# Two weight blocks at the head of the load queue, and set-up tables issued behind their rounding and subtraction

## The chip, the core and the metric

The kernel runs on one core of a Trainium2 chip. The metric is the device time of one execution in microseconds (us), median over runs. A core has TensorE (PE, matrix products; PEld is its weight load), VectorE (DVE), ScalarE (ACT), GpSimd (POOL) and SyncE (SP). SP issues most loads; ACT and POOL issue some. Each engine works through its own instructions in a fixed order, and an instruction that waits holds up everything behind it on that engine.

## The reference

Two networks follow each other on 256 tokens of width 1024. The first is a block of two layers: a norm, a projection to 3072 columns, differential and block attention, an output projection, and a convolutional feed-forward part. The second has one layer with a recurrent mixer and one with neighbourhood attention, with a second stream of 256 context tokens and modulation vectors that are computed from `w_ada`. What the change touches is the beginning:

```python
for i in range(DEPTH):
    h = rms_norm(x, ln_attn_g[i])
    dq, dk, dv, mq, mk, mv = jnp.split(h @ w_in[i], cuts, axis=-1)
    ...
```

All of it is in float32.

## The kernel before

The tokens stand in two tiles `x[0]` and `x[1]` of 128 tokens. A product of float32 is made of three products of rounded values: an operand is split into `hi` (rounded) and `lo` (the rest), and `hi*hi`, `hi*lo` and `lo*hi` are summed. For the tokens, `norm_T` does this: per token tile two squares with a sum on ACT (`sqj`), a chain of small DVE instructions (`rstd`), the scaling `xn` (one half on DVE, one on ACT), transposes on PE (`nT`), and then `ah` on ACT and `al` on DVE. The transposes for one part of the width need both token tiles. For the weights, `weights` does it: a load `raw` of a block (512 KB in this lane), the rounding `whi` on ACT (L265), and the subtraction `wlo` on DVE or, every second block, on POOL (L269).

`proj` multiplies the tokens by such blocks. The projection of layer 0 has six parts of 512 columns; each takes 4 blocks of 256 rows, 48 matmuls in all (`prj`, L292 to L294).

Around it, `setup_first` and `setup_second` build small tables: `oh`, `fl`, `rb` and `lam` are loads that ACT issues, POOL issues four loads (`b_sink`, `a_w2`, `a_a2`, `a_g2`) and clears `state`. A second lane of work, the context (`context1`), loads blocks of 128 KB of `w_in_even`, and `ada` multiplies blocks of `w_ada` (`adaw`, L778), transposes the result (`adaT`, L784), adds it up on DVE (L786, L787) and transposes two of the sums once more (`adaR`, L798).

The order in which instructions stand on each engine is not written by hand. A scheduler sorts all instructions of the program by priority and by its own estimate of times; `issue_after(i)` keeps what stands under it behind instruction i, and `high_priority()` puts what stands under it ahead. So a change at the start can move instructions far behind it. Loads of SP and ACT share eight counters in turn: a load that takes a counter waits until the load that had it before has landed, and it waits on the engine that issues it.

Of the kernel before, what the change touches and what calls it, by code (L numbers as in the profile page):

```python
# [10 lines left out]
F32 = mybir.dt.float32  # L11
F32R = mybir.dt.float32r
I32 = mybir.dt.int32
AF = mybir.ActivationFunctionType
OP = mybir.AluOpType
# [136 lines left out]
class Lane:  # L152
# [3 lines left out]
    def __init__(self, net, name, counts, named, banks, weights):  # L156
        self.net, self.name, self.counts, self.named = net, name, counts, named
        self.banks, self.weights = banks, weights
# [30 lines left out]
class Net:  # L189
# [67 lines left out]
    def weights(self, L, src, a, b):  # L257


        nc = self.nc  # L260
        raw = L.tile("raw", [128, a, b], F32, "raw")
        for p, ap in (src if isinstance(src, list) else [(slice(0, 128), src)]):
            nc.sync.dma_start(raw[p], ap)
        hi = L.tile("whi", [128, a, b], F32R, "whi")
        nc.scalar.activation(hi, raw, AF.Copy)  # L265
        lo = L.tile("wlo", [128, a, b], F32R, "wlo")
        L.blocks += 1
        eng = nc.gpsimd if L.blocks % L.nth == 0 else nc.vector
        eng.tensor_tensor(lo, raw, hi.bitcast(F32), op=OP.subtract)  # L269
        return hi, lo  # L270

    def plain_rows(self, w):

        return lambda k, a, n0, n: w[k * 128:(k + a) * 128, n0:n0 + n].rearrange("(a p) f -> p a f", p=128)

    def proj(self, L, act, rows, n0, n, ps, k0=0, nk=8, by_tile=False):


        nc = self.nc
        hi, lo = act  # L280
        a = L.weights // 512
        blocks = range(k0, k0 + nk, a)
        ready = {kb: self.weights(L, rows(kb, a, n0, n), a, n) for kb in blocks} if by_tile else {}
        for kb, t in [(kb, t) for t in range(2) for kb in blocks] if by_tile else \
                [(kb, t) for kb in blocks for t in range(2)]:
            if kb not in ready:
                ready[kb] = self.weights(L, rows(kb, a, n0, n), a, n)
            wh, wl = ready[kb]
            for k in range(a):
                ah, al = hi(kb + k, t), lo(kb + k, t)  # L290
                st, en = kb + k == k0, kb + k == k0 + nk - 1
                nc.tensor.matmul(ps[t][:, :n], ah, wh[:, k], start=st, stop=False)  # L292
                nc.tensor.matmul(ps[t][:, :n], ah, wl[:, k], start=False, stop=False)  # L293
                self.last = nc.tensor.matmul(ps[t][:, :n], al, wh[:, k], start=False, stop=en)  # L294
# [259 lines left out]
    def first_layer(self, i, x, act=None):  # L554
        nc, I, L = self.nc, self.I, self.lat
        w_in = self.plain_rows(I["w_in"][i])
        act = act or self.first_norm(i, x)
# [6 lines left out]

        def project(n):
            ps = [L.pA("prj"), L.pA("prj")]
            self.proj(L, act, w_in, n * 512, 512, ps)
            return ps

        def qkv(n, jq):  # L570

            qa, qb = self.pad_q(L)
            self.q_T(L, self.head_norm(L, project(n)), self.qg8[:, 2 * i + jq:2 * i + jq + 1], qa, qb)
            yield
            kT = L.big([128, 4, 256], name="kT")
            self.k_T(L, self.head_norm(L, project(n + 1)), self.col(f"qkg{i}", 2 * jq + 1), kT)
            yield
            ps = project(n + 2)
            v = L.big([128, 2, 512], name="v")
            for t in range(2):  # L580
                nc.scalar.activation(v[:, t], ps[t], AF.Copy)
            yield qa, qb, kT, v
# [95 lines left out]
        act = self.fns(his, los)  # L678
        for n in range(2):
            ps = [L.pA("wo"), L.pA("wo")]  # L680
# [1082 lines left out]
def run(tc, I, out, colw, cstw, keep):  # L1763
    nc = tc.nc
    with ExitStack() as ctx:
        net = Net(tc, I)
        net.pools(ctx)
        net.setup(colw, cstw, keep)
        x = [net.keep([128, D], F32, name=f"x{t}") for t in range(2)]
        for t in range(2):  # L1770
            nc.sync.dma_start(x[t], I["x"][0, t * 128:(t + 1) * 128])
        act=net.first_norm(0, x)
        net.setup_first()
        net.setup_second()
        net.context1()
        net.first_layer(0, x, act)
        net.conv_ffn(0, x)
        net.rest()
        act1=net.first_norm(1, x)
        net.first_layer(1, x, act1)  # L1780
        net.side()
        net.conv_ffn(1, x)
        net.second_block(x)
        net.store_x(x, out[0])
# [38 lines left out]
```

## Time and profile before

| what | us |
|---|---|
| median of 3 runs (2079.45 to 2088.85) | 2084.95 |
| profiled execution, its own time | 2083.04 |
| its span, first to last instruction | 2081.2 |
| PE busy in the span | 1908.7 |

PE is busy in 92% of the span, so the kernel is bound by PE, and time is lost where PE waits. The profile gives the start of each instruction in us from the start of the span.

### The profile page before, as it was taken

To read this page: it belongs to the slowest core of one execution; us is meant where nothing else is said; L and a number is where in the kernel's file an instruction comes from. 1 tells how busy PE (TensorE), PEld (TensorE's weight loads), DVE (VectorE), ACT (ScalarE), POOL (GpSimd) and SP (SyncE) were. 2 spreads that over 40 slices of the span, in tenths; PEclk is the share of its full clock that TensorE was granted. 3 is DMA by queue.
4 is the path that set the end of the run, shared out by engine and by line. 5 is a ranking of instruction groups with operands and counts; after the bars stand their busy time and mean duration, and the time that the engine had idled before them with its cause. 6 is when DMAs were issued, how large, how long until landed. Compare 5 with 4: busy or idle time off the path is not lost. (4 is left out here: it accounts for less than half of the span.)

```text
span 2081.2 us, 37712 instructions
## 1 busy us (share of the span) xinstructions
PE 1908.7 (92%) x14178; PEld 1592.7 (77%) x14178; DVE 1369.1 (66%) x2855; ACT 1025.4 (49%) x1990; POOL 928.4 (45%) x621
## 2 busy tenths in 40 slices
PE   6989999989998889999898888998699989998998
PEld 4567868888665458899797777887599977777997
DVE  5575378856687555786679878557764468656444
ACT  4455455545454435465456553334454454654443
POOL 3235544693232444544545355446255454113453
PEclk9999999999999999999999998899899999998999
DMA  9957455445455565664573334427465526234562
GB/s 341 310 173 232 153 181 167 151 141 169 131 185 178 190 199 168 198 218 152 163 219 103 102 110 150 127 71 235 158 204 177 178 100 220 78 105 154 181 200 73
DMA packets 270815, 351.08 MB, mean 169 GB/s; under 512 B 43150, under 2 KB 195469, under 8 KB 270632
## 3 DMA queue, kind: packets, MB, share of 16 engines
q1 hardware_dynamic: 267992, 343.32, 51.9%
q0 software_dynamic: 1968, 4.33, 0.7%
q8 instruction: 112, 1.84, 0.4%
q10 hardware_dynamic: 672, 1.02, 0.1%
q14 instruction: 71, 0.58, 0.1%
HBM read 334.04 MB, written 14.55 MB: 167 GB/s over the span
## 5 line engine op out<-in xcount | busy, mean ns | idle before, releaser
L269 POOL TENSOR_TENSOR wlo<-raw,whi 128x1024 fp32r<-128x1024 f32 (+2 forms) x408 | 781.7, 1931 | 982.2 <-ACT whi L265 809.2
L265 ACT ACTIVATE whi<-raw 128x1024 fp32r<-128x1024 f32 (+2 forms) x600 | 507.8, 882 | 142.8 <-issue 35.0
L269 DVE TENSOR_TENSOR wlo<-raw,whi 128x1024 fp32r<-128x1024 f32 x192 | 305.4, 1591 | 108.2 <-ACT whi L265 94.2
L308 PE MATMUL f<-ah,whi 128*128 128x256 f32 x768 | 225.8, 294 | 15.2 <-ACT whi L265 14.5
L310 PE MATMUL f<-ah,wlo 128*128 128x256 f32 x768 | 226.8, 295 | 7.6 <-POOL wlo L269 7.6
L309 PE MATMUL f<-al,whi 128*128 128x256 f32 x768 | 225.4, 294 | 0.5 <-DVE al L383 0.5
L746 PE MATMUL acc<-whi,hh 128*128 128x512 f32 x432 | 168.3, 393 | 2.1 <-ACT hh L461 2.1
L747 PE MATMUL acc<-wlo,hh 128*128 128x512 f32 x432 | 169.2, 392 | 0.0
L308 PEld LDWEIGHTS f<-ah,whi 128*128 128x128 f32 x768 | 153.6, 200 | 19.2 <-ACT whi L265 15.7
L748 PE MATMUL acc<-whi,hl 128*128 128x512 f32 x432 | 165.3, 391 | 0.4 <-DVE hl L462 0.4
L310 PEld LDWEIGHTS f<-ah,wlo 128*128 128x128 f32 x768 | 153.7, 200 | 11.7 <-POOL wlo L269 8.7
L309 PEld LDWEIGHTS f<-al,whi 128*128 128x128 f32 x768 | 153.8, 200 | 3.0 <-DVE al L383 0.9
L1584 DVE TENSOR_TENSOR r<-r 128x512 f32<-128x512 f32 x48 | 41.2, 858 | 129.4 <-ACT r L1583 128.3
L1583 ACT ACTIVATE r<-f 128x512 f32<-128x512 f32 x48 | 28.7, 598 | 179.2 <-PE f L310 179.0
L293 PE MATMUL prj<-wlo,ah 128*128 128x512 f32 (+1 forms) x272 | 108.2, 399 | 2.7 <-DVE wlo L269 1.6
L292 PE MATMUL prj<-whi,ah 128*128 128x512 f32 (+1 forms) x272 | 108.9, 406 | 0.4 <-DVE bt L499 0.4
L310 PE MATMUL g<-ah,wlo 128*128 128x256 f32 x352 | 102.1, 290 | 6.3 <-POOL wlo L269 6.3
L294 PE MATMUL prj<-whi,al 128*128 128x512 f32 (+1 forms) x272 | 106.2, 398 | 1.4 <-DVE al L383 1.4
L778 PE MATMUL ada<-adaw,kept 128*32 128x512 f32 x384 | 96.8, 636 | 8.6 <-DMA adaw<-in_w_ada_dram 8.3
L308 PE MATMUL g<-ah,whi 128*128 128x256 f32 x352 | 102.7, 292 | 0.4 <-DVE kept L786 0.4
L310 PE MATMUL up<-ah,wlo 128*128 128x256 f32 x352 | 101.4, 288 | 1.2 <-POOL wlo L269 1.2
L309 PE MATMUL g<-al,whi 128*128 128x256 f32 x352 | 102.3, 291 | 0.0
(473 smaller groups left out, 4861.2 us busy)
## 6 DMA issues: line engine op xcount, KB each, us to landing
raw<-in_w_ff_dram SPq DMA_DIRECT2D x128, 512.0 KB, 4.1
raw<-in_w_up_dram SPq DMA_DIRECT2D x88, 512.0 KB, 4.6
adaw<-in_w_ada_dram SPq DMA_DIRECT2D x144, 256.0 KB, 5.0
raw<-in_w_ff_dram SPq DMA_DIRECT2D x128, 256.0 KB, 3.9
raw<-in_w_in_dram SPq DMA_DIRECT2D x48, 512.0 KB, 4.7
raw<-in_w_down_dram SPq DMA_DIRECT2D x44, 512.0 KB, 4.1
adaw<-in_w_ada_dram SPq DMA_DIRECT2D x24, 512.0 KB, 7.3
raw<-in_w_out_dram SPq DMA_DIRECT2D x24, 512.0 KB, 4.4
```

What stands on the lines that cost most here:

```text
L265: nc.scalar.activation(hi, raw, AF.Copy)
L269: eng.tensor_tensor(lo, raw, hi.bitcast(F32), op=OP.subtract)
L292: nc.tensor.matmul(ps[t][:, :n], ah, wh[:, k], start=st, stop=False)
L293: nc.tensor.matmul(ps[t][:, :n], ah, wl[:, k], start=False, stop=False)
L294: self.last = nc.tensor.matmul(ps[t][:, :n], al, wh[:, k], start=False, stop=en)
L308: nc.tensor.matmul(pv[:, j], wh[:, k % a, c], ah, start=first, stop=False, skip_group_check=skip)
L309: nc.tensor.matmul(pv[:, j], wh[:, k % a, c], al, start=False, stop=False, skip_group_check=skip)
L310: nc.tensor.matmul(pv[:, j], wl[:, k % a, c], ah, start=False, stop=k == 7, skip_group_check=skip)
L746: nc.tensor.matmul(acc[t][n], hh[:, k, c], wh[:, n], start=st, stop=False)
L747: nc.tensor.matmul(acc[t][n], hh[:, k, c], wl[:, n], start=False, stop=False)
L748: self.last = nc.tensor.matmul(acc[t][n], hl[:, k, c], wh[:, n], start=False, stop=en)
L778: nc.tensor.matmul(ps[32 * j:32 * j + 32], self.sT[:, k], raw[:, k - kb], start=k < 4, stop=k >= 4)
```

## The change

`first_weights` takes the first two blocks of the first projection out of `proj` and asks for them with high priority ahead of the set-up. `proj` then finds them in `ready`. `setup_first` is issued after the rounding of the second block (`rounded`, on ACT), `setup_second` after its subtraction (`rest_of`, on POOL).

```diff
+    def first_weights(self):
+        rows, a = self.plain_rows(self.I["w_in"][0]), self.lat.weights // 512
+        with self.tc.high_priority():
+            self.ahead = {kb: self.weights(self.lat, rows(kb, a, 0, 512), a, 512) for kb in range(0, 2 * a, a)}
+        return self.rounded.ins, self.rest_of.ins
...
-        ready = {kb: self.weights(L, rows(kb, a, n0, n), a, n) for kb in blocks} if by_tile else {}
+        ready = {kb: self.weights(L, rows(kb, a, n0, n), a, n) for kb in blocks} if by_tile else ready or {}
...
-            self.proj(L, act, w_in, n * 512, 512, ps)
+            self.proj(L, act, w_in, n * 512, 512, ps, ready=self.ahead if i == n == 0 else None)
...
         act=net.first_norm(0, x)
-        net.setup_first()
-        net.setup_second()
+        rounded, rest_of = net.first_weights()
+        with tc.issue_after(rounded):
+            net.setup_first()
+        with tc.issue_after(rest_of):
+            net.setup_second()
         net.context1()
```

Lines below the new function move by 8 (in `run` by 11). The built program shows what the scheduler makes of it.

The first loads that SP issues, before. `kept` is the place of `x` here, `raw_3411`, `raw_3429`, `raw_3447` and `raw_3465` are the four blocks of the first projection, and `DMAHWn` is counter n.

```order
L1771 DMA kept_58<-in_x_dram 128x1024 x2
L263 DMA raw_459<-in_w_in_even_dram 128x256
L263 DMA raw_3411<-in_w_in_dram 128x2x512
L263 DMA raw_471<-in_w_in_even_dram 128x256 [waits DMAHW0_49]
L263 DMA raw_483<-in_w_in_even_dram 128x256 [waits DMAHW2_49]
L263 DMA raw_3429<-in_w_in_dram 128x2x512 [waits DMAHW3_49]
L263 DMA raw_3447<-in_w_in_dram 128x2x512 [waits DMAHW4_49]
```

The same of the change, where the first two blocks are `raw_155` and `raw_161`.

```order
L263 DMA raw_155<-in_w_in_dram 128x2x512
L263 DMA raw_161<-in_w_in_dram 128x2x512
L1779 DMA kept_58<-in_x_dram 128x1024 x2
L263 DMA raw_471<-in_w_in_even_dram 128x256
L263 DMA raw_483<-in_w_in_even_dram 128x256
L263 DMA raw_495<-in_w_in_even_dram 128x256 [waits DMAHW0_49]
L783 DMA adaw_6655<-in_w_ada_dram 128x512 [waits DMAHW1_49]
L783 DMA adaw_6658<-in_w_ada_dram 128x512 [waits DMAHW2_49]
L263 DMA raw_3447<-in_w_in_dram 128x2x512 [waits DMAHW4_49,DVE_49]
```

The two blocks stand ahead of the tokens, not behind them, and the third block has two loads of `w_ada` ahead of it.

ACT's start before; the first two loads, `cols` and `consts`, stand ahead of these rows in both programs.

```order
L340 ACTIVATE sqj_82,ss_81<-kept_58 128x512 [waits DMAHW1_49]
L340 ACTIVATE sqj_84,ss_81<-kept_58 128x512
L503 DMA lam_217<-in_diff_lambda_dram 128x512
...
L363 ACTIVATE xn_97<-kept_58,rstd_86 128x512 [waits DVE_49]
L340 ACTIVATE sqj_101,ss_100<-kept_58 128x512 [waits DMAHW2_49]
L340 ACTIVATE sqj_103,ss_100<-kept_58 128x512
L475 DMA rb_159<-in_rel_bias_dram 32x12 [waits DMAHW2_49,Activation_49]
L265 ACTIVATE whi_3413<-raw_3411 128x1024 [waits DMAHW6_49]
L363 ACTIVATE xn_116<-kept_58,rstd_105 128x512 [waits DVE_49,Activation_49]
```

ACT's start with the change.

```order
L265 ACTIVATE whi_157<-raw_155 128x1024 [waits DMAHW1_49]
...
L265 ACTIVATE whi_163<-raw_161 128x1024 [waits DMAHW2_49]
L478 DMA oh_167<-in_consts_dram 32x256 [waits DMAHW3_49]
L511 DMA lam_229<-in_diff_lambda_dram 128x512 [waits DMAHW5_49]
L481 DMA fl_169<-in_consts_dram 128x128 [waits DMAHW7_49]
L348 ACTIVATE sqj_82,ss_81<-kept_58 128x512 [waits DMAHW4_49]
...
L265 ACTIVATE whi_473<-raw_471 128x256 [waits DMAHW6_49,Activation_49]
L265 ACTIVATE whi_485<-raw_483 128x256 [waits Activation_49]
L483 DMA rb_171<-in_rel_bias_dram 32x12 [waits DMAHW4_49]
L265 ACTIVATE whi_3449<-raw_3447 128x1024
L371 ACTIVATE xn_116<-kept_58,rstd_105 128x512 [waits DVE_49]
```

Two roundings and three loads now stand ahead of the first square of the tokens. `lam` waits for counter 5, which `x[1]` has, and `fl` for counter 7, which `raw_483` has. `rb` waits for `raw_3447`, and the third block's rounding stands behind it.

PE before, between the last matmuls of the fourth part of the projection (`prj_3779`) and the first of the fifth (`prj_3934`).

```order
L294 MATMUL prj_3779<-whi_3836,al_80 128x512
L528 MATMUL S_3903<-kT_3521,qa_3405 128x128
...
L784 MATMUL adaT_350<-kept_58,asb_348 128x128 x4
L784 MATMUL adaT_6715<-kept_58,asb_6713 128x128 x4
L798 MATMUL adaR_6722<-kept_58 8x128 x2
L370 MATMUL nT_405<-kept_58,xn_382 128x128
L370 MATMUL nT_418<-kept_58,xn_382 128x128
L422 MATMUL qT_3876<-kept_58,hn_3872 128x128 x4
```

The same place with the change.

```order
L302 MATMUL prj_3779<-whi_3836,al_80 128x512
L786 MATMUL ada_6731<-adaw_6744,kept_58 32x512
...
L792 MATMUL adaT_362<-kept_58,asb_360 128x128 x4
L792 MATMUL adaT_6758<-kept_58,asb_6756 128x128 x4
L378 MATMUL nT_417<-kept_58,xn_394 128x128
L378 MATMUL nT_430<-kept_58,xn_394 128x128
L786 MATMUL ada_6765<-adaw_6766,kept_58 32x512
...
L430 MATMUL qT_3876<-kept_58,hn_3872 128x128 x4
```

`adaR` has gone from here to a place some 90 rows earlier, behind eight transposes of `pB`, and nine matmuls of `ada` (four of `ada_6731` and five of `ada_6765`) have come.

## Rows read from the trace of the kernel before

**Rows 1.** The page: span, and busy time of each engine.

```profile
span 2081.2 us, 37712 instructions
PE 1908.7 (92%) x14178; PEld 1592.7 (77%) x14178; DVE 1369.1 (66%) x2855; ACT 1025.4 (49%) x1990; POOL 928.4 (45%) x621
```

**Rows 2.** Timeline of ACT: start, length, engine, line; idle time before in brackets.

```profile
5.19 0.63 ACT L340 ACTIVATE sqj<-kept 128x512 f32<-128x512 f32 x1 [1.76 <-DMA kept<-in_x_dram]
...
10.49 0.19 ACT L340 ACTIVATION_READ_ACCUMULATOR sqj<-kept 128x1 f32 x1
14.89 0.35 ACTq L475 DMA_DIRECT2D rb<-in_rel_bias_dram  x1
15.29 1.06 ACT L265 ACTIVATE whi<-raw 128x1024 fp32r<-128x1024 f32 x1 [4.61 <-DMA raw<-in_w_in_even_dram]
...
21.17 0.41 ACT L265 ACTIVATE whi<-raw 128x256 fp32r<-128x256 f32 x1
```

**Rows 3.** Timeline of all engines, the same stretch.

```profile
16.38 1.23 DVE L269 TENSOR_TENSOR wlo<-raw,whi 128x1024 fp32r<-128x1024 f32 x1 [4.11 <-ACT whi L265]
...
17.71 0.49 DVE L362 TENSOR_SCALAR xn<-kept,rstd 128x512 f32<-128x512 f32 x1
...
19.72 1.22 PE L292 MATMUL prj<-whi,ah 128*128 128x512 f32 x2
```

**Rows 4.** Windows: stretch, length, busy us by engine, PE clock, DMA share, GB/s.

```profile
0.00:3.00 3.00, 0.00 (x0) 0.00 (x0) 0.48 (x1) 0.85 (x1) 2.47 (x9) 1.00 0.36 69
3.00:6.00 3.00, 0.00 (x0) 0.00 (x0) 0.63 (x9) 1.24 (x4) 0.77 (x2) 1.00 1.03 387
6.00:8.50 2.50, 0.00 (x0) 0.00 (x0) 1.85 (x17) 0.72 (x4) 0.00 (x0) 1.00 0.99 201
```

**Rows 5.** Loads of the first 60 us: count, KB each, median us to landing.

```profile
raw<-in_w_in_dram SPq DMA_DIRECT2D x16, 512.0 KB, 6.8
...
adaw<-in_w_ada_dram SPq DMA_DIRECT2D x14, 256.0 KB, 7.1
kept<-in_x_dram SPq DMA_DIRECT2D x2, 512.0 KB, 6.3
...
raw<-in_w_in_even_dram SPq DMA_DIRECT2D x7, 128.0 KB, 8.5
...
kept<-in_consts_dram ACTq DMA_DIRECT2D x1, 336.0 KB
kept<-in_cols_dram ACTq DMA_DIRECT2D x1, 303.0 KB, 4.6
```

**Rows 6.** The tile `raw` in the first 60 us, all its loads.

```profile
DMA to landing us min/median/max: 3.8/7.3/10.7
```

**Rows 7.** Timeline of PE, first part of the projection.

```profile
26.21 1.04 PE L778 MATMUL ada<-adaw,kept 128*32 128x512 f32 x2
...
31.28 0.60 PE L477 MATMUL pB<-oh,rb 32*12 32x256 f32 x2
...
37.69 0.62 PE L292 MATMUL prj<-whi,ah 128*128 128x512 f32 x2
```

**Rows 8.** Timeline, all engines, between the fourth and fifth parts of the projection.

```profile
98.84 1.92 PE L778 MATMUL ada<-adaw,kept 128*32 128x512 f32 x16
...
101.03 0.39 PE L294 MATMUL prj<-whi,al 128*128 128x512 f32 x1
...
104.28 2.27 DVE L396 TENSOR_SCALAR hst<-hst 128x16 f32<-128x16 f32 x1
...
106.96 0.38 PE L798 MATMUL adaR<-kept 128*8 128x128 f32 x2 [3.35 <-DVE kept L787]
...
110.39 1.09 PE L422 MATMUL qT<-kept,hn 128*128 128x128 f32 x4 [1.51 <-DVE rstd L344]
...
113.40 0.63 PE L294 MATMUL prj<-whi,al 128*128 128x512 f32 x1
```

**Rows 9.** Windows: PE's granted clock, as a share of full speed, stands before the DMA share.

```profile
110.00:120.00 10.00, 9.61 (x40) 8.02 (x41) 4.79 (x16) 3.35 (x6) 0.00 (x0) 0.72 0.22 80
```

More of the change, by code (lines that the diff above doesn't have):

```diff
@@ L264, in weights @@
         hi = L.tile("whi", [128, a, b], F32R, "whi")
-        nc.scalar.activation(hi, raw, AF.Copy)
+        self.rounded = nc.scalar.activation(hi, raw, AF.Copy)
         lo = L.tile("wlo", [128, a, b], F32R, "wlo")
@@ L268, in weights, with proj @@
         eng = nc.gpsimd if L.blocks % L.nth == 0 else nc.vector
-        eng.tensor_tensor(lo, raw, hi.bitcast(F32), op=OP.subtract)
+        self.rest_of = eng.tensor_tensor(lo, raw, hi.bitcast(F32), op=OP.subtract)
         return hi, lo
+    def first_weights(self):
[3 more added lines that the diff above has]
+        return self.rounded.ins, self.rest_of.ins
     def plain_rows(self, w):
         return lambda k, a, n0, n: w[k * 128:(k + a) * 128, n0:n0 + n].rearrange("(a p) f -> p a f", p=128)
-    def proj(self, L, act, rows, n0, n, ps, k0=0, nk=8, by_tile=False):
+    def proj(self, L, act, rows, n0, n, ps, k0=0, nk=8, by_tile=False, ready=None):
         nc = self.nc
```

## The prediction

> **What bounds the kernel now.** I read the page first: PE is busy in 1908.7 of 2081.2 us [rows 1], so the time moves only where PE's waits move. Those that the change can reach are at the start, so I went through the timelines of the first 40 us, ACT's first, then DVE's and PE's.
>
> The first matmul of the projection starts at 19.72 [rows 3]. The chain behind it runs as follows. ACT squares the first token tile from 5.19 on and has finished the second tile's squares at 10.49 + 0.19 = 10.68 [rows 2], 5.49 us later. What comes next on ACT is the issue of the small load `rb`, and that comes only at 14.89, since its counter belongs to a load of `w_in_even` that has not landed. ACT stands idle 4.61 us for it, and the rounding of the first weight block starts behind it at 15.29, 1.06 long [rows 2]. DVE has that block's subtraction ahead of the last `rstd` step, so it waits 4.11 us, subtracts for 1.23, and scales the second tile at 17.71 [rows 3]. From there to the first matmul it is 19.72 - 17.71 = 2.01 us. So before, the tokens are early and the weights hold them up: a late `rb` on ACT costs some 4 to 5 us. That is what the change could win.
>
> **The start with the change.** The order shows that the two blocks are loaded ahead of the tokens and not behind them. It also shows that ACT's first square now stands behind the loads `oh`, `lam` and `fl`, and that `fl` waits for the counter of `raw_483`, the eighth load. So the squares start when eight loads have landed: two weight blocks and two token tiles of 512 KB, `cols` with 303, `consts` with 336 and two context blocks of 128 [rows 5], 2943 KB or 3.01 MB. By 3.0 us the core has moved 3 x 69 = 0.21 MB, and then 387 GB/s as long as it has loads in flight [rows 4]. That gives 3.0 + (3.01 - 0.21) / 0.387 = 10.2 us. Between 6.0 and 8.5 the rate before was only 201 GB/s [rows 4], at a time when SP stood waiting for counters. If such a stretch comes back it costs 2.5 x (387 - 201) / 387 = 1.2 us, so 11.4. These are the two bounds. POOL's four loads don't stand in the sum, because they now come behind POOL's first subtraction.
>
> The Trainium skill ("DMA: Bandwidth & Descriptors", section Specifications) gives a core about 358 GB/s from HBM. By it the eight loads would land at an estimated 10.8 us. The rows of this case hold 387 GB/s over 3 us, so the measured rate decides.
>
> From the start of the squares the steps are those of before. The second tile's squares end 5.49 later, at 15.7 to 16.9. ACT rounds two context blocks (0.41 each [rows 2]), which ends at 16.5 to 17.7. Then `rb` is issued, which waits for the third block, `raw_3447`. Ahead of that block on SP stand one more context block and two loads of 256 KB, so 0.13 + 0.52 + 0.52 MB more have to land, and of `lam` and POOL's loads at most another 1 MB. That is 4.2 to 5.2 MB, or 13.3 to 15.9 by the same rate, and 17.1 with the slow stretch: just hidden behind ACT's own work. The rounding of the third block (1.06) then ends at 17.6 to 18.8, and DVE, which again has a subtraction ahead of the scaling, is through 1.23 later, 18.8 to 20.0. With the 0.10 to the scaling and 2.01 to the first matmul it starts at 20.9 to 22.1, which is **1.2 to 2.4 us later than before**. The wait that the change removes from the first block comes back at the third.
>
> What is won is behind that. With the change, the first 48 matmuls of the projection have no `ada` among them. Before, they had six in three pieces of which one is 1.04 long [rows 7], 3.1 in all, and a table's matmul of 0.60 [rows 7]. The first part took from 19.72 to 37.69, 17.97 us; without these it is 14.3, and ends at 35.2 to 36.4. But the six (twelve rows of the profile at 1.92 / 16 = 0.12 [rows 8], 1.4 us) and the table (0.6 at most) only move back. So PE stands at 37.2 to 38.4 for equal work against 37.69: -0.5 to +0.7, **+0.1** as the middle. The blocks themselves are no limit there: two are split before the tokens are, the third sets the start, and the fourth lands 0.52 MB, or 1.4 us, behind the third.
>
> **Moved and hidden.** POOL's memset and four loads stand behind a subtraction; their tables are wanted only by the context's mixer and the attention with a sink, far behind the first projection. DVE's clearing of `line` and the bias tables come later too, and the attention that reads them stands behind three parts of the projection; PE has that work as cover. If it ran out, the softmax of the first head would be late. I take both at nothing.
>
> **The place at 103 us.** Between two parts of the projection PE waits for a norm on DVE. From the last matmul at 101.03 to `qT` at 110.39 it is 9.36 us; in them PE waits 3.35 for `adaR` and 1.51 for `qT` [rows 8]. With the change `adaR` (0.38) is gone and nine `ada` (18 rows of 0.12, 2.2 us) stand there. If DVE's chain takes as long as before, PE has done 2.2 - 0.4 = **1.8 us** more in the same wait. The bounds: 0 if these loads come late, and 3.35 + 1.51 if the chain also gets shorter; one of its small instructions took 2.27 there [rows 8]. I take 1.8, since the wait for the norm's last step stays in both orders.
>
> **The rest.** By the order, PE's instructions stand otherwise in the first 16% of the program, between 20% and 40% and between 62% and 76%, and alike elsewhere. What moved there are single steps past each other. I take them at nothing on balance; a place like the one at 103 us, more or less, is what they can be worth.
>
> Sum: 2083.04 + 0.1 - 1.8 = 2081.3 against the profiled execution. The median of the runs stands 1.9 above that execution, so I give **2083.2**.
>
> **The rivals.**
>
> *Faster by over 0.5% (10.4 us, about what a measurement of this kernel can tell from no change), so below 2074.5.* The place at 103 us goes altogether. Then PE wins 3.35 + 1.51 = 4.9, and the slow matmuls behind the wait too: PE's clock is granted at 0.72 on average from 110 to 120 [rows 9], so partly at its lower level of 1.2 GHz, and ten matmuls took 0.63 where 0.39 is usual [rows 8], 2.4 us. That is 7.3 in place of 1.8, so 2077.7; it decides from 10.5 on, that is if one more wait of the size of `adaR`'s (3.35) goes with it, at 2074.3. For it speaks that `adaR` has left. Against it speaks that `qT` still waits for the same norm. Chance 0.16.
>
> *Slower by over 0.5%.* The token tiles land late, because they are behind the blocks, and ACT stands behind three loads' counters. The longest landing of a block was 10.7 us [rows 6]. If the first token tile, whose counter the third block takes, lands only with the rest of the eight at 11.4, and the third block 10.7 later at 22.1, its rounding ends at 23.2 and the first matmul starts at 23.2 + 1.23 + 0.10 + 2.01 = 26.5, 6.8 later than before; 1.7 of that is won back in the first part as above, so 5.1 stand in the sum where 0.1 stood, and the time is 2088.2. It decides beyond the bound if the third block lands after 29 us. For it speaks that this block has more loads ahead of it than the first block had; against it that the longest landing belongs to a stretch in which SP, ACT and POOL all loaded, and POOL's loads come later now. To all that is slower by over 0.5% I give 0.18.
>
> *The change does not do what it says:* the blocks are early, but the start is set by the tokens and by `rb` on another block, and everything behind is as before: the start's 1.2 to 2.4 stays lost and nothing is won later, 2084.95 + 1.8 = 2086.8. That is inside the bound, and so counts with my forecast; chance 0.25, and 0.41 for the forecast itself.
>
> **The numbers.** Same 0.66, faster 0.16, slower 0.18. The range reaches from 2071 (the faster rival with 3.35 twice) to 2096 (the slower one with 7.3 for one more place like that at 103 us): 0.1 is left out at each end.
>
> **What would show it.** Right: the first square of ACT at 10.2 to 11.4 in place of 5.19; `rb` issued after 16; the first matmul of the projection at 20.9 to 22.1; 48 matmuls of it without `ada` between them, done by about 36; at some 100 us `ada` where `adaR` was, and a wait for `qT` still there. Wrong: the first matmul before 19 or after 24; a first wait of ACT that ends well before the eighth load; PE waits in the later stretches that differ by more than 10 us in sum, which I could not foresee.

## The result and the profile after

The changed kernel takes 2119.08 us (median of 4 runs, 2115.29 to 2126.22) against 2085.11 for the kernel before: a ratio of 1.0168, with a 95% interval of 1.0148 to 1.0188. It is slower by 34 us, where I forecast 2083.2 and gave 0.18 to "slower". The profiled execution took 2126.22, the longest of the four and 7.1 over their median, so its waits add up to more than the 34.

The page of the changed kernel, span and engines, which answers to [rows 1]:

```profile
span 2124.4 us, 37719 instructions
PE 1924.4 (91%) x14178; PEld 1599.5 (75%) x14178; DVE 1366.4 (64%) x2855; ACT 1027.6 (48%) x1990; POOL 928.8 (44%) x621
```

PE waits longer, 2124.4 - 1924.4 = 200.0 us where it was 172.5, and for the same 14178 matmuls it is also busy 15.7 longer. Timeline of all engines at the start, the rows that answer to [rows 2, 3]:

```profile
11.55 0.63 ACT L348 ACTIVATE sqj<-kept 128x512 f32<-128x512 f32 x1 [2.76 <-DMA raw<-in_w_in_even_dram]
...
16.53 0.19 ACT L348 ACTIVATION_READ_ACCUMULATOR sqj<-kept 128x1 f32 x1
16.62 0.71 ACT L265 ACTIVATE whi<-raw 128x256 fp32r<-128x256 f32 x2
25.35 0.33 ACTq L483 DMA_DIRECT2D rb<-in_rel_bias_dram  x1
25.73 1.06 ACT L265 ACTIVATE whi<-raw 128x1024 fp32r<-128x1024 f32 x1 [8.40 <-DMA adaw<-in_w_ada_dram]
...
26.82 1.23 DVE L269 TENSOR_TENSOR wlo<-raw,whi 128x1024 fp32r<-128x1024 f32 x1 [8.32 <-ACT whi L265]
...
27.96 0.48 DVE L370 TENSOR_SCALAR xn<-kept,rstd 128x512 f32<-128x512 f32 x1
...
29.97 0.80 PE L300 MATMUL prj<-whi,ah 128*128 128x512 f32 x1
```

Up to 17.33 it goes as forecast. Then ACT stands 8.40 us ahead of `rb`, and the view names a load of `w_ada`, not the third block, `raw_3447`, which I had named ahead of the prediction as what `rb` waits for. The uses of `rb`'s counter 4, from the waits in the built program and the counter's records in the trace (times in us; each use waits until the one above it has landed):

```
use 1  x[0]        issued  1.76  landed  9.08
use 2  raw_3447    issued  9.16  landed 14.30   (the third block)
use 3  adaw_6667   issued 14.84  landed 25.33   (w_ada, fifth load)
use 4  rb          issued 25.35
```

So the third block was there at 14.30, and `rb` waited for the use behind it. The first matmul comes at 29.97, 10.25 later than in [rows 3].

The rest of the loss is spread. One place, timeline of PE between the third and the fourth part of the projection:

```profile
76.49 1.91 PE L786 MATMUL ada<-adaw,kept 128*32 128x512 f32 x12
...
78.50 0.27 PE L506 MATMUL pB<-fl,hk 128*128 128x128 f32 x1
...
82.07 2.29 PE L786 MATMUL ada<-adaw,kept 128*32 128x512 f32 x4 [2.64 <-DMA adaw<-in_w_ada_dram]
85.05 1.11 PE L792 MATMUL adaT<-kept,asb 128*128 128x128 f32 x4 [0.69 <-ACT asb L788]
...
86.17 0.42 PE L506 MATMUL pB<-fl,hk 128*128 128x128 f32 x1
```

A wait of 2.64 for `w_ada`, and behind it the same matmul of `pB` takes 0.42 where it took 0.27. The granted clock fell there to its lower level of 1.2 GHz. Windows as in [rows 9], changed kernel, where PE's clock is 0.83:

```profile
80.00:100.00 20.00, 17.25 (x81) 7.43 (x82) 4.34 (x10) 5.10 (x9) 4.07 (x6) 0.83 0.90 310
```

The same 20 us of the kernel before, where it is 1.00:

```profile
80.00:100.00 20.00, 20.00 (x98) 12.49 (x102) 8.93 (x35) 7.95 (x21) 3.88 (x3) 1.00 0.77 273
```

PE's waits over the whole span, changed kernel: total, times, longest.

```profile
PE nT L378 <- DVE xn L370: 49.8, 11, 15.2
PE ada L786 <- DMA adaw<-in_w_ada_dram: 15.2, 8, 4.5
...
PE nT L378 <- DVE cf L1570: 5.8, 1, 5.8
...
PE f L318 <- DVE wlo L269: 4.6, 1, 4.6
```

The same view of the kernel before has these rows for the first two, and no row for the other two:

```profile
PE nT L370 <- DVE xn L362: 37.4, 10, 9.9
...
PE nT L370 <- DMA kept<-in_consts_dram: 10.0, 1, 10.0
PE ada L778 <- DMA adaw<-in_w_ada_dram: 8.3, 5, 3.3
```

Ahead of the first matmul PE stood 27.8 us in two waits for `xn`, where it was 10.0 for `consts` and 7.6 for `xn`. So 10.2 of the 27.5 us of added waiting are the start. `w_ada` adds 6.9, and two single places that the old order did not have add 10.4. The `xn` waits behind the start are 7.8 shorter (22.0 against 29.8), and many small ones make up the rest: a new order makes and removes waits all over the program.

### The profile page after: what moved, and what is told of

Its sections match the earlier page's. It is cut to its first block, busy times and chain, and to the rows that moved or that the text cites. A ratio compares the mean times of both kernels' runs of the same rounds, so it can differ in the third digit from the quotient of the medians.

```text
span 2124.4 us, 37719 instructions
## 1 busy us (share of the span) xinstructions
PE 1924.4 (91%) x14178; PEld 1599.5 (75%) x14178; DVE 1366.4 (64%) x2855; ACT 1027.6 (48%) x1990; POOL 928.8 (44%) x621
## 5 line engine op out<-in xcount | busy, mean ns | idle before, releaser
L1592 DVE TENSOR_TENSOR r<-r 128x512 f32<-128x512 f32 x48 | 36.1, 752 | 127.2 <-ACT r L1591 126.1
```

## The experiments

All times are medians, with the kernel before measured beside them; behind a ratio stands its 95% interval. "Rows of PE" are matmuls in the built order; the program has 11921.

### Is it `rb` at the start?

In the changed kernel (`rb_sp`) and in the kernel before (`before_rb_sp`):

```diff
-        nc.scalar.dma_start(rb, I["rel_bias"])
+        nc.sync.dma_start(rb, I["rel_bias"])
```

> The changed kernel with one edit: the small load rb is issued by SP, not by ACT. PE's order stays row for row, and DVE, ACT and SP differ by this one place. In the changed kernel ACT stood 8.40 us before rb, and rb waited not for the third block (landed at 14.3) but for a later load of w_ada on the same counter (landed at 25.33). Theory 'start': without that wait the third block is rounded at 17.4, and the first matmul of the projection starts at 21.9 to 22.9 in place of 30.2; the time falls by 7 to 9, to 2110 to 2112. Rival 'absorbed' (the later stages wait for DVE and POOL anyway and take the start's loss back): 2116 to 2120. Rival 'all from the start' (the other waits grow out of it): below 2095.

> The kernel before with the same single edit, rb issued by SP; PE's order is that of before row for row. By the prediction's reading a late rb costs 4 to 5 us: first matmul of the projection at about 15.5, time 2080 to 2081. Theory 'the block was late too': the first block's last packet counted at 14.01, so the rounding can begin 1.26 earlier and no more; first matmul at 18.4 to 18.6, time 2083.5 to 2084.5, not told from before.

`rb_sp`: 2111.73, ratio 1.0123 (1.0100 to 1.0146), 7.4 less than the changed kernel. Timeline, all engines:

```profile
18.05 1.23 DVE L269 TENSOR_TENSOR wlo<-raw,whi 128x1024 fp32r<-128x1024 f32 x1
...
19.38 0.49 DVE L370 TENSOR_SCALAR xn<-kept,rstd 128x512 f32<-128x512 f32 x1
...
21.39 0.80 PE L300 MATMUL prj<-whi,ah 128*128 128x512 f32 x1
```

Without that wait the first matmul starts at 21.39, 0.5 ahead of the range in the expectation. So the wait is worth some 7 us, and 25.7 are left. `before_rb_sp`: 2085.50, ratio 0.9998 (0.9985 to 1.0012); first matmul at 19.17. The prediction's reading that a late `rb` cost 4 to 5 us before falls: the first block's counter was complete only at 14.01, so there was 1.3 to win at most.

### Which part of the change, and is an engine held?

`no_gates` drops both `issue_after`; `behind_tokens_no_gates` drops the priority too; `behind_tokens_rb_sp` drops the priority only and has `rb` on SP:

```diff
-        with self.tc.high_priority():
+        if True:
             self.ahead = ...
...
-        with tc.issue_after(rounded):
-            net.setup_first()
-        with tc.issue_after(rest_of):
-            net.setup_second()
+        net.setup_first()
+        net.setup_second()
```

> The change without its two issue_after: only the two weight blocks are early. rb still stands on ACT behind the same w_ada load, and the set-up table's matmul pB has 67 projection matmuls ahead of it on PE (70 in the changed kernel, 28 before). Theory 'table and rb' (the loss is rb on ACT and the late pB, which holds DVE's copy of line for 11.4 us and through it ACT and POOL): the loss stays, 2110 to 2122. Rival 'gates' (the late set-up on POOL and DVE causes it): 2083 to 2095.

> The two blocks without high priority, so behind the tokens on SP, both gates kept, and rb issued by SP. pB has 24 projection matmuls ahead of it. Some PE rows stand otherwise than before in as many places as in the changed kernel. Theory 'table and rb': both causes are gone, first matmul at 18 to 22, DVE waits less than 4 us for pB, time 2080 to 2092. Rival 'any new order costs' (the loss behind the start comes from the reordered stretches and not from one held engine): 2100 to 2112.

> Only the first two blocks asked for ahead of the set-up, without priority and without gates: tokens, block 1, block 2 on SP; rb on ACT waits for the third block; pB has 24 projection matmuls ahead (28 before). Start as before or up to 2 us earlier, first matmul at 17.5 to 20. Theory 'held engines': nothing is held longer than before, 2080 to 2090. Rival 'the order': some 2100 of 11923 PE rows stand otherwise than before, 2098 to 2112.

2127.98, 2107.66 and 2099.69, ratios 1.0209 (1.0187 to 1.0231), 1.0104 (1.0083 to 1.0125) and 1.0060 (1.0039 to 1.0080). `no_gates` is above its expected range: the gates are not the cause. A start that is as good as before (first matmul at 19.75 in the second of them, 19.62 in the third) helps, but 21.6 and 14.0 are still lost. Next, the tables. `table_early` is the changed kernel with the loads of `oh` and `rb` taken out of the set-up and put first of all; `table_early_behind` and `table_early_nogates` are the same without priority and without gates, `before_table_early` is the kernel before with this one edit, and `tables_first_before` writes the whole set-up ahead of the norm:

```diff
+    def setup_table(self):
+        ...
+        nc.scalar.dma_start(oh, I["consts"][0:32, at:at + n])
+        nc.scalar.dma_start(rb, I["rel_bias"])
...
+        net.setup_table()
         act=net.first_norm(0, x)
```

> The changed kernel (two blocks ahead of the tokens, both gates) with the loads of oh and rb taken out of setup_first and issued first of all on ACT. rb then waits for no counter, and the table's matmul pB stands first on PE instead of behind 70 projection matmuls, so DVE's copy of line is done before the projection. Theory 'held engines': the loss of the changed kernel is rb on ACT (7.4 measured) and then DVE and ACT held behind pB (6.6 us for the squares' sums, 4.7 for the next roundings, with rb on SP); both are gone, first matmul at 20 to 23, PE's stretch from 40 to 120 us as before within 4 us, time 2085 to 2097. Rival 'the order': what the scheduler makes of any other start costs some 20 us in many small waits and slow matmuls behind them; 2103 to 2115.

> As table_early, but the two blocks without high priority: on SP the first token tile, block 1, the second token tile, block 2. ACT's first square waits for the first token tile alone. fl on ACT waits for the second w_ada load ahead of the third block's rounding, which I estimate to land at 13 to 15 by the loads ahead of it at 387 GB/s. Theory 'held engines': first matmul at 17 to 20, time 2078 to 2090. Rival 'the order': 2100 to 2112, though the start is as good as before or better.

> The kernel before with the set-up written ahead of the first norm, so oh, rb and lam are the first small loads and pB is the first matmul; the weight blocks come where they came. No weight block is early and nothing waits for pB. Theory 'held engines': 2078 to 2092. Rival 'the order' (any reshuffle of this size costs, whatever the change): 2098 to 2115.

> The kernel before with oh and rb loaded first on ACT, as in table_early, but without early weight blocks and without gates. pB has no projection matmul ahead of it; first matmul at 18 to 20. If table_early's time (2080.8) comes from the tables alone: 2076 to 2084. Theory 'the order' says only that the rows between 500 and 900 us decide: 455 rows in 2500 to 4500 that table_early keeps as before (113 moved there) are about 980 moved here, so 2093 to 2113, with the loss between 550 and 900 us.

> table_early (2080.8) without its two gates. Start as there: first matmul at 18 to 20, no engine held for pB. If the gates matter by what they hold back (POOL's four loads and its clearing come early again, 0.77 MB ahead of other loads, some 2 us): 2081 to 2085. Theory 'the order': about 880 of the rows 2500 to 5000 stand otherwise than before (113 in table_early), 2093 to 2113, with the loss between 550 and 900 us.

`table_early`: 2080.82, ratio 0.9973 (0.9956 to 0.9989), below both ranges of its expectation and the one version that beats both kernels, the one before by 4.9 us. Timeline of ACT, DVE and PE:

```profile
8.07 0.63 ACT L348 ACTIVATE sqj<-kept 128x512 f32<-128x512 f32 x1 [0.17 <-DMA kept<-in_x_dram]
...
10.48 0.41 DVE L493 COPY line<-pB 12x256 f32<-12x256 f32 x1
...
18.65 0.80 PE L300 MATMUL prj<-whi,ah 128*128 128x512 f32 x1
```

The squares wait for their own tile, the copy of `line` from the table's `pB` is done ahead of the projection, and PE is 1.07 ahead of [rows 3] at its first matmul. The others, in the order of the expectations, take 2112.99, 2117.97, 2104.41 and 2099.00 (ratios 1.0121, 1.0140, 1.0079 and 1.0058, with intervals of at most 0.0025 to each side). First matmul of the projection in `table_early_behind`:

```profile
19.17 0.80 PE L300 MATMUL prj<-whi,ah 128*128 128x512 f32 x1
```

and in `before_table_early`:

```profile
20.18 1.22 PE L292 MATMUL prj<-whi,ah 128*128 128x512 f32 x2
```

The first starts 0.55 ahead of the kernel before and still loses 27; the second starts 0.46 behind it and loses 17. In these two "held engines" at the start is not enough. The other two decide less: `table_early_nogates` starts at 21.50, 1.8 late, and `tables_first_before` at 57.31. It works off `ada` first, with PE waiting 13.8 us for loads of `w_ada` in the first 60, so that a worse start may be part of its loss. Of the five ranges that the rival "the order" gave, two held, two were passed by 1 and 3 us, and `table_early` speaks against it.

`bias_act` issues the store `bias_line` on ACT:

```diff
-        nc.sync.dma_start(scr, line)
+        nc.scalar.dma_start(scr, line)
```

> As rb_sp (2111.7), with one more edit: the store bias_line, which waits for DVE's copy of line, is issued by ACT, not by SP. PE, DVE and POOL stand row for row as in rb_sp. There SP stood 4.28 us before this store, with weight blocks and w_ada loads behind it, and PE later waits 4.5 us in 2 for w_ada. Theory 'held load queue': those loads come some 4 us earlier, the waits for w_ada between 60 and 150 us shrink, and the time falls by 3 to 8, to 2104 to 2109. Rival 'buffers': the block behind the store waits for POOL to free a buffer anyway (SP stands 4.50 for it next), 2110 to 2113.

2112.64, ratio 1.0117 (1.0092 to 1.0142), as `rb_sp`, in the range of the rival "buffers". It doesn't decide: the hold only moved to the next load. SP's waits in `rb_sp`, 30 to 55 us:

```profile
SPq L491 <- DVE lp L514: 4.1, 1, 4.1
```

and in `bias_act`:

```profile
SPq L1504 <- DVE lp L514: 4.1, 1, 4.1
```

### Is it the order?

`mid_side` only writes the second layer's side lane ahead of that layer:

```diff
-        net.first_layer(1, x, act1)
-        net.side()
+        net.side()
+        net.first_layer(1, x, act1)
```

> The kernel before with net.side() (a side lane's modulation blocks) written ahead of the second layer instead of behind it. PE's first 2500 rows, some 480 us, stand row for row as before; some 970 of the rows 2500 to 5000 and some 640 between 7500 and 9500 stand otherwise; the start and its loads are untouched and the same work is done. Theory 'the order' (the interleaving that the scheduler finds between 500 and 900 us is worth some 20 us by itself): no difference up to 480 us, then 8 to 28 later by 900 us; 2095 to 2113. Rival 'held engines at the start' (only what starts there counts): 2082 to 2089.

2089.10, ratio 1.0011 (0.9994 to 1.0028): an order of its own in the middle cost nothing that can be told. So "any new order costs" is wrong as a rule; whether a given order costs had to be tried by itself. The next kernels hold PE's rows in a written order by edges that keep the issue order alone; `order` is a table taken from the other built kernel, and `lo` and `hi` choose the stretch. The scheduler then sorts the other engines and SP's loads around these rows:

```diff
+    pe = [i for i in tc.nc.cur_bb.bb.instructions if i.engine == mybir.EngineType.PE]
+    for a, b in zip(order[lo:hi], order[lo + 1:hi]):
+        tc.add_manual_dep(pe[b], pe[a].name, mybir.DependencyInfo(
+            mybir.DependencyClass.NoSync, mybir.DependencyReason.DATA), reason="pin")
```

> The changed kernel with rb issued by SP (rb_sp, 2111.7), and with all 11921 matmul rows of PE held in the order of the kernel before by edges that keep the issue order and wait for nothing else. The early blocks, both gates and the moved set-up loads stay. DVE then has 83 rows otherwise than before and ACT 43, where rb_sp has 1292 and 454. Theory 'PE's order' (the loss of 25.7 that rb_sp still has comes from the order that the scheduler chose): 2080 to 2089. Rival 'the loads' (early blocks and late set-up hold up what PE needs, in any order): 2100 to 2112.

> As pin_all, but only the rows from 2000 on (some 400 us) are held in the order of before; the first 2000 stand as in rb_sp, 499 of them otherwise than before. By rb_sp's profile 11 of its loss stood by 450 us. Theory 'the first stretch' alone: 2107 to 2112. Theory 'both stretches': 2094 to 2103. If the order behind 400 us is all: 2080 to 2089.

> The complement: the first 2000 rows of PE in the order of before, the rest as the scheduler then puts it, some 1650 rows otherwise than before, most of them between 500 and 900 us. Theory 'the first stretch' alone: 2080 to 2089. Theory 'both stretches': 2090 to 2101. If the order behind 400 us is all: 2105 to 2112. An own order of the middle was free in mid_side (2089.1), which speaks for the first.

> As pin_all, but rb stays on ACT, where it waits for the second block of the second part, which I estimate to land at 24 to 26. It differs from pin_all by this wait alone. ACT stands some 8 us for it. Theory: the first matmul of the projection starts at 29 to 31, and 5 to 9 us of it reach the end: 2087 to 2097, that much above pin_all. Rival 'absorbed': as pin_all within 2.

> The kernel before, with its own loads, blocks, tables and no gates, but all 11921 matmul rows of PE held in the order that they have in the changed kernel (the same edges as in pin_all). Tokens first, rb as early as before within 2 us, first matmul at 19 to 22. Theory 'PE's order': by pin_all (2094.7) against rb_sp (2111.7) the order is worth 17, so 2099 to 2111. Rival 'order and loads only together' (this order costs only with the changed loads): 2083 to 2092.

> As pin_all (2094.7), with DVE from row 60, ACT from row 40 and POOL from row 14 on also held in the order of before; 16 rows of DVE, 20 of ACT and 4 of POOL still stand otherwise, all at the start, and 71 of SP. pin_all's profile is level with before up to 600 us and loses 7 between 620 and 700, where 36 rows of DVE stand otherwise. Theory 'the order, of the other engines too': 2083 to 2090. Rival 'the loads' (the remaining 9.6 comes from the early blocks and from SP's order): 2092 to 2097.

| kernel | early blocks and gates | PE's order | `rb` | median | before | ratio |
|---|---|---|---|---|---|---|
| `rb_sp` | yes | changed | SP | 2111.73 | 2086.07 | 1.0123 (1.0100 to 1.0146) |
| `pin_all` | yes | before | SP | 2094.65 | 2085.09 | 1.0049 (1.0035 to 1.0064) |
| `pin_four` | yes | before, also DVE, ACT, POOL | SP | 2089.05 | 2085.84 | 1.0024 (1.0009 to 1.0039) |
| `pin_after` | yes | before | ACT | 2102.44 | 2085.09 | 1.0084 (1.0069 to 1.0098) |
| `order_of_after` | none | changed | ACT | 2107.88 | 2085.84 | 1.0105 (1.0088 to 1.0121) |
| `pin_late` | yes | before from row 2000 on | SP | 2112.29 | 2085.09 | 1.0129 (1.0113 to 1.0146) |
| `pin_early` | yes | before up to row 2000 | SP | 2107.89 | 2085.09 | 1.0129 (1.0110 to 1.0147) |

This is shown both ways. The changed order put onto the kernel before, without early blocks and gates, loses 22.0; the early blocks and gates in the old order of four engines lose 3.2. `pin_all`, with PE's rows alone held, lies between its two ranges, and `pin_four` is 5.6 below it. So "the order" is that of the whole program and not of PE's rows alone. The loads belong to it: in `order_of_after` the first thirteen loads of SP are those of the kernel before, but behind them SP's order follows PE's: counted in the built programs, 194 of its 1094 loads and stores would have to move to stand as in the kernel before, and 40 to stand as in the changed one. Whether PE's rows or the loads that follow them do the harm, no run here separates. `order_of_after` also has the place of 82 us (a wait of 3.79 for `w_ada`, and `pB` at 0.42 behind it): timeline of PE.

```profile
75.36 2.61 PE L778 MATMUL ada<-adaw,kept 128*32 128x512 f32 x4 [3.79 <-DMA adaw<-in_w_ada_dram]
78.70 1.12 PE L784 MATMUL adaT<-kept,asb 128*128 128x128 f32 x4 [0.73 <-ACT asb L780]
...
79.82 0.42 PE L498 MATMUL pB<-fl,hk 128*128 128x128 f32 x1
```

`pin_after` stands 7.8 above `pin_all`, the wait for `rb` again. ACT there:

```profile
24.81 1.06 ACT L265 ACTIVATE whi<-raw 128x1024 fp32r<-128x1024 f32 x1 [7.38 <-DMA raw<-in_w_in_dram]
```

`pin_late` lands at the edge of the range for "the first stretch alone", and `pin_early` in the range for "the order behind 400 us is all". The two exclude each other, so none of the three theories stands: either half of the new order costs about as much as the whole. Which rows do it stays open, but the profiles show where it begins. Compared at equal work of PE (the time so far, less waits and less half of the time at the lower clock), `rb_sp` and `order_of_after` are 10 us behind the kernel before where that one stands at 90 us, of 17 each at the end. `pin_early` is 1 behind there and 23 at the end, and `pin_four` is level in both places.

## Why the prediction was wrong, point by point

**The squares** were to start at 10.2 to 11.4; they start at 11.55. The loads moved 398 GB/s from 3 to 6 us and 395 from 6 to 11.2, near the 387 that I took from [rows 4], and the eighth load's counter was complete at 11.15; then `fl` was still to be issued (0.33). The Trainium skill's 358 GB/s ("DMA: Bandwidth & Descriptors", section Specifications) is below both rates, and the measured ones decide. **The second tile** was to be done at 15.7 to 16.9: 16.72. **The third block** was to land at 13.3 to 15.9: 14.30.

**"`rb` ... waits for the third block, ... just hidden": the step that failed first.** The order names the counter and not the use of it that is awaited. The use was the next one, a `w_ada` load of which I had no term. With this term alone taken out, `rb_sp` starts its first matmul at 21.39, within the 20.9 to 22.1 forecast. The slower rival had the place (ACT held by a counter) but the wrong load: its third block at 22.1 never came, so that its direction came true was luck. The wait cost 7.4 (`rb_sp`) and 7.8 (`pin_after`).

**"What is won is behind that": this step held.** Timeline of PE, changed kernel, which answers to [rows 7]:

```profile
42.59 0.39 PE L302 MATMUL prj<-whi,al 128*128 128x512 f32 x1
42.81 0.39 PE L301 MATMUL prj<-wlo,ah 128*128 128x512 f32 x1
...
45.31 0.39 PE L302 MATMUL prj<-whi,al 128*128 128x512 f32 x1
45.63 1.05 PE L786 MATMUL ada<-adaw,kept 128*32 128x512 f32 x2
```

Sixty matmuls of the projection, 48 of the first part and 12 of the second, stand ahead of the first `ada`. The 48th is the row at 42.59, and the next starts at 42.81, 12.84 after the first, where I had 14.3 and the kernel before took 17.97. With the 2.0 that only moved back, PE is 7.1 behind the kernel before at equal work, after 10.25 at the start. So 3.1 was won back where I had 1.7; the late start hid it.

**The place at 103 us, where I had 1.8 gained: this step failed too.** Timeline of PE, changed kernel, which answers to [rows 8]:

```profile
119.69 0.39 PE L302 MATMUL prj<-whi,al 128*128 128x512 f32 x1
...
127.62 0.66 PE L378 MATMUL nT<-kept,xn 128*128 128x128 f32 x2 [3.49 <-DVE rsq_t L252]
128.21 3.21 PE L786 MATMUL ada<-adaw,kept 128*32 128x512 f32 x10
131.35 0.66 PE L430 MATMUL qT<-kept,hn 128*128 128x128 f32 x4
```

`adaR` has gone and 18 rows of `ada` have come, as the order said. But from the last matmul to `qT` it is 11.66 where it was 9.36. Eight rows of `ada` stand ahead of the wait (1.07 in all), and the ten behind it take 3.21, where I priced all 18 at 2.2. So 2.3 us more went by for the 1.8 of work that I had counted as hidden. More work in a wait won nothing, since a wait of 3.49 still stood there (3.35 before) and the clock had fallen (0.87 granted from 120 to 130).

**"The rest": "nothing on balance" was the step that cost most.** By `order_of_after` the order is worth 22.0, and by `rb_sp` against `pin_four` 22.7. My last sentence named PE waits that differ by over 10 us in sum as what I could not foresee; that is what came. Step by step from `after` over `rb_sp` and `pin_four` to before, 7.4 are `rb`, 22.7 the order and 3.2 what is left, 33.3 of 34.0. These add up by their making, and with medians of 4 to 12 runs each is good to a few us; `pin_after` and `order_of_after` are what bears them out from the other side. The 3.2 may be the early loads or the few rows that still stand otherwise; that is open.

**Why a reordered row costs more than its wait** can be seen when each span is taken apart: the span, less the time in which PE does nothing, less half of the time in which it works at its lower level of 1.2 GHz. From the matmul records and the granted clock of each profile:

```
kernel            span    idle   busy at 1.2 GHz   span - idle - half of that
before            2081.2  172.5      108.6             1854.4
after             2124.4  200.0      141.2             1853.8
rb_sp             2099.4  187.0      115.7             1854.6
no_gates          2134.5  202.3      157.4             1853.6
order_of_after    2101.1  183.6      121.7             1856.7
pin_four          2080.1  172.6      107.5             1853.8
table_early       2078.2  170.8      102.7             1856.0
behind_tokens_rb_sp
                  2108.6  182.1      141.3             1855.8
table_early_behind
                  2110.9  182.7      129.0             1863.7
```

The last column is 1851 to 1864 in all 20 profiles, and within 3 us of the kernel before in these but `table_early_behind`: PE's work at full clock is nearly the same in each kernel, and what differs is mostly waiting and the lower clock. After against before that is 27.5 and 16.3. The Trainium skill ("TensorE: Matmul & The Clock Gate", section "HAM oscillation — how this bites in real kernels") also charges half of the time at the lower level; the nearly constant column agrees. (The profiles of `rb_sp`, `order_of_after` and `pin_four` are among the shortest of their runs, and that of the changed kernel is the longest, so the sums above go by medians.)

## What to carry to other kernels

An early load is bought with its place in every queue: follow each small load behind it to the exact use of its counter, by counting the uses, since an engine that issues it stands there with all its other work. Where a scheduler sorts the program, price a change at the start with the whole new order, not with its own rows: here what is left with the old order held cost some 3 us, a wait for a counter 7, and the order 22, and the 18 variants lay between 2081 and 2128. Hold the old order on the engines by issue edges, and try the change in it, before a time is put down to the change.

## What was not expected of the hardware

The added waiting of the changed kernel came with more loss by the lower clock, 16.3 us for 27.5. That is no rate: in `rb_sp` it is 3.6 for 14.5, in `behind_tokens_rb_sp` 16.4 for 9.6. Behind a wait of 2.64 the matmuls of `pB` took 0.42 in place of 0.27, while behind the 2.31 for `qT` at 63 us those of `prj` took 0.39 as elsewhere. And a `w_ada` load of 256 KB, issued at 14.84 among other loads, landed 10.5 us later, when a 512 KB block issued at 9.16 had taken 5.1: eleven loads issued before it were still under way then, four of them POOL's, which the gate had moved there. The core moved 372 GB/s from 14.84 to 25.33, so the load stood behind others and not in a slow stretch.
